# One weight tile in four split by ScalarE and an accumulating DMA, and two small reorderings, in an encoder layer on one core

## The chip, the cores and the metric

The kernel runs on one core of one Trainium2 chip. The metric is the device time of one execution in microseconds (us), the median of three runs. TensorE is called PE below, its weight loads PEld, VectorE DVE, ScalarE ACT, GpSimd POOL and SyncE SP. SP issues the plain DMAs.

## The reference, cut to what matters

The program is one layer of a bidirectional encoder, run on a prompt of 512 tokens and a sample of 256, each behind 16 meta tokens, with a model width of 1024, all in float32:

```python
h = h + 0.5 * swiglu(rmsnorm(h, ffn1_norm_w), ffn1_w_gate, ffn1_w_up, ffn1_w_down)   # width 2816
u = rmsnorm(h, mix_norm_w)
q, k, v, z, xbc, dt = split(u @ w_in)
h = h + concat([diff_attention(q, k, v), ssd_mixer(z, xbc, dt)]) @ w_out
h = h + 0.5 * swiglu(rmsnorm(h, ffn2_norm_w), ffn2_w_gate, ffn2_w_up, ffn2_w_down)
return rmsnorm(h, final_norm_w)[meta tokens dropped]
```

`diff_attention` has 8 heads with two score maps each; `ssd_mixer` is a chunked state-space scan in both directions over chunks of 128 tokens.

## The kernel before, in words

**Float32 by three products.** PE multiplies float32r, a rounded float32. So every operand is kept as a big part `hi` (the rounded value) and a small part `lo` (what the rounding left), and a product is the sum of three matmuls, hi·hi, lo·hi and hi·lo, in that order (`mm3`, lines 320 to 322). `split` (lines 184 to 186) makes the two parts of a weight tile: ACT casts the raw tile into `hi` (L185), DVE subtracts `hi` from the raw tile into `lo` (L186).

**Weights.** They stream from HBM through the class `Weights`. A raw tile `wr` is 512 rows by 256 columns, stored as 128x1024 (512 KB), in two buffers, loaded by SP (L212). Its two parts lie in `wh` and `wl`, four buffers each. `jobs` is the list of splits in the order of use; `pump` makes one further split whenever a buffer has been freed.

**The feed-forward layers** are cut into groups of column pairs (`GROUPS`). The first group is computed plainly. In each later one `quad` computes a 2x2 block product by seven products of quarter size in place of eight; a quad is run for the gate weights and one for the up weights of each pair of column tiles. Its four weight jobs are `a` (one quarter), `b` and `d` (sums of quarters, made by DVE in the tile `sums`, L258 to L264, before their split) and `c` (the second raw tile as it is). The products run as p1 (needs `a`), then p4 of the quad before, p6 and p5 (need `b`), p2 (needs `c`), p7 and p3 (need `d`), and p4 (needs `c` again), which is put off behind the next quad's p1. One product is 12 matmuls of 392 columns (384 in the second layer). After each group `down` adds its part of the down projection.

**Between the layers** the input projection runs, and beside it, in a generator advanced a step at a time between the projection's matmuls, the state-space scan (`seq`, from line 1178). Each of its rounds, two to a chunk, loads three 512 KB tiles of rows of `ar_d` spread over the partitions (`load_ab`, L1212 and L1216), masks two on POOL (L1236), takes exponentials on ACT (L1240, L1241), three elementwise passes on DVE (L1243 to L1245), and multiplies on PE (L1253, L1256). The tiles come from the pool `w4` of 15 buffers, which the scan shares with its states, its transposed inputs and the rest of the stage.

**Parameters.** The generator `parameters` waits 30 rounds, loads 18 small pieces by SP (L854 to L863), waits 4 rounds, transposes the packed vectors on PE (L876), and multiplies and sums the four lambda vectors on DVE (L880, L881).

**What sets the order.** The framework's planner orders each engine's queue at build time: instructions have their priority from the program's order, and one that is ready early by the planner's own estimate of times may be put ahead of others. On the chip each engine then works through its queue in that fixed order. `behind(ins)` ties instructions to come after `ins` on the same engine.

Of the kernel before, what the change touches and what calls it, by code (L numbers as in the profile page):

```python
# [10 lines left out]
AF = mybir.ActivationFunctionType  # L11
ALU = mybir.AluOpType
PSUM = bass.MemoryType.PSUM

P = 128
# [24 lines left out]
LAM_INIT = 0.8 - 0.6 * math.exp(-0.0)  # L40
# [7 lines left out]
def body(tc, x_prompt, x_sample, meta_tokens, ffn1_norm_w, ffn1_w_gate, ffn1_w_up, ffn1_w_down,  # L48
# [3 lines left out]
    nc = tc.nc  # L52
    V = nc.vector
    S = nc.scalar
    G = nc.gpsimd
# [51 lines left out]
    def ps_x():  # L107
        return pp.tile([P, 512], F32, tag="x", name="ps_x", bufs=2)
# [10 lines left out]
    ident = const.tile([P, P], F32, name="ident")  # L119
# [15 lines left out]
    raws_in = []  # L135
    jobs = []
# [44 lines left out]
            plan_1(("o", part, cp), w_out0, k0, 4, 256 * cp, 256)  # L181
    plan_ffn(2, ffn2_w_gate[0], ffn2_w_up[0], ffn2_w_down[0])

    def split(hi, lo, src):
        a = S.copy(hi, src)  # L185
        return a, V.tensor_tensor(lo, src, hi.bitcast(F32), ALU.subtract)  # L186

    @contextmanager
    def behind(ins):

        with ExitStack() as st:
            for i in ins:
                st.enter_context(tc.issue_after(i.ins))
            yield
# [5 lines left out]
    class Weights:  # L200
        raw, ready = {}, {}
# [42 lines left out]
        def split_fast(self, key, kind, raw, hi, lo):  # L244

            x, y = slice(0, P), slice(P, 2 * P)
            if kind == "c":
                ins = split(hi, lo, raw[0])
                self.ready[key] = [[(hi[:, i, c], lo[:, i, c]) for i in range(4)] for c in (x, y)]
                return ins  # L250
            hv, lv = (t.rearrange("p a b -> p (a b)").rearrange("p (s k f) -> p s k f", s=2, k=4) for t in (hi, lo))
            if kind == "a":
                ins = split(hv[:, 0], lv[:, 0], raw[0][:, :, x])
            else:
                if kind == "b":
                    sums = stretch_pool[0].tile([P, 2 * 4 * P], F32, tag="sums", name="sums", bufs=1)
                    t = self.sums = sums.rearrange("p (s k f) -> p s k f", s=2, k=4)
                    V.tensor_tensor(t[:, 1], raw[0][:, :, y], raw[1][:, :, y], ALU.add)  # L258
                    V.tensor_tensor(t[:, 0], t[:, 1], raw[0][:, :, x], ALU.add)
                else:  # L260

                    t, self.sums = self.sums, None
                    V.tensor_tensor(t[:, 1], raw[0][:, :, x], raw[0][:, :, y], ALU.add)
                    V.tensor_tensor(t[:, 0], t[:, 0], raw[1][:, :, x], ALU.add)  # L264
                ins = split(hv, lv, t)
            self.ready[key] = [[(hv[:, q, i], lv[:, q, i]) for i in range(4)] for q in range(1 if kind == "a" else 2)]
            return ins
# [45 lines left out]
            done()  # L313

    last_mm = [None]

    def mm3(ps, a, b, start, stop, onto=False):

# [180 lines left out]
    def ffn(f, h, halves, norm, after, last, new_g, new_up, first, parts=None, rms=None, ended=None):  # L499
# [145 lines left out]
        def d_unit(ws, k0, m, part):  # L645
            o, n = part
            ps = ps_any()
            dense(ps[:, :n], ws, m % 2, [g_t[k0 + i] for i in range(len(ws))], o, n)
            dst = h[m][:, o:o + n]
            V.scalar_tensor_tensor(dst, ps[:, :n], 0.5, dst, ALU.mult, ALU.add)  # L650

        def down(g):
            k0 = 2 * bounds[g]
# [134 lines left out]
    ps = ps_s()[:, 0, :]  # L788
# [7 lines left out]
    for js in ((0, 1, 2), (3, 4, 5), (6, 7)):  # L796
        ps = (ps_x if js[0] == 3 else ps_mm)()
# [4 lines left out]
        with behind([a]):  # L802
            for j in js:
                ins = put_h(js[0] == 3, j, at[j - js[0]], 0, C0)
# [47 lines left out]
    def parameters():  # L852
        def rep(dst, src, n):
            nc.sync.dma_start(out=dst, in_=src.partition_broadcast(n))  # L854

        for _ in range(30):
            yield 1
        V.memset(prm, 0.0)
        for (src, n), a in zip(rows, offs):
            nc.sync.dma_start(out=prm[a:a + n, :], in_=src.rearrange("(k p) -> k p", p=P))  # L860
        nc.sync.dma_start(out=prm[cw0:cw0 + 70, :], in_=conv_w[0].rearrange("t (k p) -> (t k) p", p=P))
        nc.sync.dma_start(out=prm[sub0:sub0 + 1, :], in_=attn_subln_w[0:1])
        nc.sync.dma_start(out=rbT, in_=rel_bias.rearrange("b h -> h b"))  # L863
        for j in range(2):
            rep(dvec[64 * j:64 * j + 64, :], ssm_d[0].rearrange("(m j) -> j m", j=2)[j], 64)
        rep(dtb[:, 0:16], dt_bias_fwd[0], P)
        rep(dtb[:, 16:32], dt_bias_bwd[0], P)
        rep(nega[:, 0:16], a_log_fwd[0], P)
        rep(nega[:, 16:32], a_log_bwd[0], P)
        lqk = [small([P, P], "B", 4).rearrange("p (i d) -> p i d", i=2) for _ in range(2)]  # L870
        for i, src in enumerate((lambda_q1, lambda_k1, lambda_q2, lambda_k2)):
            rep(lqk[i // 2][:, i % 2, :], src[0], P)
        for _ in range(4):
            yield 1
        ps = ps_x()
        nc.tensor.transpose(ps[:, :P], prm, ident)  # L876
        V.tensor_copy(prmT, ps[:, :P])
        V.tensor_scalar(subw, prmT[:, sub0:sub0 + 1], 1.0 - LAM_INIT, None, ALU.mult)
        for i in range(2):
            V.tensor_tensor(lqk[i][:, 0, :], lqk[i][:, 0, :], lqk[i][:, 1, :], ALU.mult)  # L880
            V.reduce_sum(lam2[:, i:i + 1], lqk[i][:, 0, :], mybir.AxisListType.X)  # L881
        yield 1

    def distances():
# [291 lines left out]
    def seq(chunks, meta_col):  # L1176
# [31 lines left out]
        def load_ab(c, g):  # L1208
            ab = []
            for d in range(2):  # L1210
                t = w4(D).rearrange("p (h t) -> p h t", h=8)
                nc.sync.dma_start(out=t, in_=ar_d[d, 8 * g:8 * g + 8, P * c:P * c + P].partition_broadcast(P))  # L1212
                ab.append(t)
            ea = w4(D).rearrange("p (h t) -> p h t", h=8)
            for d in range(2):
                nc.sync.dma_start(out=ea[64 * d:64 * d + 64],  # L1216
                                  in_=ar_d[d, 8 * g:8 * g + 8, P * c:P * c + P].partition_broadcast(64))
            ab_q.append((ab, ea))

        for i, c in enumerate(chunks):  # L1220
            col = CH[c]
            kk = 128 if i < L - 1 else 64
            X = Xs[c]
            ps = ps_s()
            for g in range(2):
                nc.tensor.matmul(ps[:, g, :P], xbc[8][64 * g:64 * g + 64, col:col + P],
                                 xbc[9][64 * g:64 * g + 64, col:col + P], start=True, stop=True)
            cb = ssm["row"][:, 416:672].rearrange("p (g t) -> p g t", g=2)
            S.copy(cb, ps[:, :, :P])
            for g in range(2):  # L1230
                load_ab(c, g)
                yield 1
                ab, ea = ab_q.pop(0)
                for d in range(2):
                    step = 1 - 2 * d
                    G.affine_select(out=ab[d], in_=ab[d], compare_op=ALU.is_ge, fill=NEGBIG, base=0,  # L1236
                                    pattern=[[0, 8], [step, P]], channel_multiplier=-step)
                    for h in range(8):
                        col_s = 16 * d + 8 * g + h
                        S.activation(ab[d][:, h, :], ab[d][:, h, :], AF.Exp, bias=ssm["asp"][:, c, col_s:col_s + 1])  # L1240
                S.activation(ea, ea, AF.Exp)  # L1241
                yield 1
                V.tensor_tensor(ea, ea, ssm["cdup"][g][:, col:col + P].unsqueeze(1).to_broadcast([P, 8, P]), ALU.mult)  # L1243
                V.tensor_tensor(ab[0], ab[0], ab[1], ALU.add)
                V.tensor_tensor(ab[0], ab[0], cb[:, g, :].unsqueeze(1).to_broadcast([P, 8, P]), ALU.mult)  # L1245
                yield 1
                ps = ps_x()
                for j in range(4):
                    o = [ps[64 * e:64 * e + 64, j * P:(j + 1) * P] for e in range(2)]
                    for e in range(2):  # L1250
                        h = 2 * j + e
                        hh = 8 * g + h
                        nc.tensor.matmul(o[e], X[:, 64 * hh:64 * hh + 64], ab[0][:, h, :], start=True, stop=False)  # L1253
                    for e in range(2):
                        h = 2 * j + e
                        nc.tensor.matmul(o[e], H[i][:kk, g, 64 * h:64 * h + 64], ea[:kk, h, :], start=False, stop=True)  # L1256
                for j in range(4):
                    m = 4 * g + j
                    V.scalar_tensor_tensor(xbc[m][:, col:col + P], xbc[m][:, col:col + P], dvec[:, m:m + 1],
                                           ps[:, j * P:(j + 1) * P], ALU.mult, ALU.add)  # L1260
# [450 lines left out]
```

## Time and profile before

| | |
|---|---|
| median of 3 runs (lowest to highest) | 1845.69 us (1845.63 to 1845.99) |
| the profiled execution | 1846.13 us |
| its span, first to last instruction | 1844.4 us |
| mean granted PE clock | 0.988 |
| PE busy, PEld busy | 97%, 93% of the span |
| DVE, ACT, POOL busy | 70%, 43%, 5% |
| DMA | 169.75 MB, mean 92 GB/s |

The span is cut by stages in the windows below. Matmuls overlap in the record, so a matmul shows some 340 ns of its own while the next one starts 0.17 to 0.18 us later; what PE loses shows as idle time before an instruction and in the granted clock.

### The profile page before, as it was taken

Reading aid. Unit: us, or ns where it says so; the run is one execution under the profiler, and the core shown is the slowest. Engines: PE = TensorE matmul, PEld = TensorE weight load, DVE = VectorE, ACT = ScalarE, POOL = GpSimd, SP = SyncE. Lnnn points to the kernel's source line nnn. Section 1 sums busy time; section 2 is a strip of 40 time slices with the busy share of each in tenths; the row PEclk is TensorE's granted clock in tenths of the full one; section 3 lists DMA queues with packets and bytes.
Section 4 is the critical chain, followed back from the end, with each engine's and each line's share of the span. In section 5 each row is a group of like instructions: output and inputs, shape, how many; then the busy total and the mean of one; then the engine's idle time right before and its main releaser. Section 6 shows DMA issues by size and latency. Waiting matters only on the chain.

```text
span 1844.4 us, 27371 instructions
## 1 busy us (share of the span) xinstructions
PE 1790.5 (97%) x10718; PEld 1719.0 (93%) x10718; DVE 1296.1 (70%) x2511; ACT 797.8 (43%) x1564; POOL 93.8 (5%) x118
## 2 busy tenths in 40 slices
PE   7999999999999999999899999999999999999998
PEld 6999999999998898878899898999999999999997
DVE  6857858686766697667788888674877575757573
ACT  5523414232333453668367676343433232424244
POOL 0000000000011000224100000001100000000002
PEclk8999999999999999999899999999999999999999
DMA  4212222212222523877431325321123121212121
GB/s 144 69 46 69 65 73 58 80 58 76 59 88 91 164 73 114 221 200 216 152 99 60 101 77 190 99 101 32 35 80 91 46 90 47 89 45 87 47 79 69
DMA packets 161268, 169.75 MB, mean 92 GB/s; under 512 B 9921, under 2 KB 146234, under 8 KB 161138
## 3 DMA queue, kind: packets, MB, share of 16 engines
q1 hardware_dynamic: 161122, 168.00, 30.3%
q8 instruction: 84, 1.38, 0.3%
q14 instruction: 46, 0.38, 0.1%
q10 hardware_dynamic: 16, 0.00, 0.0%
HBM read 148.54 MB, written 22.87 MB: 93 GB/s over the span
## 4 chain that ended last, share of the span: by engine, by line
PE 78%; DVE 11%; ACT 4%; DMA 4%; issue 2%; SPq 1%; POOL 0%; DVEq 0%; POOLq 0%; ACTq 0%
PE ps_mm L320 12%; PE ps_mm L322 11%; PE ps_mm L321 11%; PE ps_x L320 8%; PE ps_x L322 8%; PE ps_x L321 8%; PE ps_s L320 4%; PE ps_s L321 4%; PE ps_s L322 4%; DVE w L1056 2%; PE ps_s L1493 2%; DVE wl L186 2%; ACT w L1240 1%; PE ps_s L1611 1%; DMA w<-ar_d 1%
## 5 line engine op out<-in xcount | busy, mean ns | idle before, releaser
L320 PE MATMUL ps_mm<-w,wh 128*128 128x384 f32 (+3 forms) x1296 | 441.1, 340 | 5.2 <-ACT w L185 2.1
L321 PE MATMUL ps_mm<-w,wl 128*128 128x384 f32 (+3 forms) x1296 | 438.7, 338 | 1.7 <-DVE wl L186 1.7
L322 PE MATMUL ps_mm<-w,wh 128*128 128x384 f32 (+3 forms) x1256 | 426.2, 340 | 2.8 <-DVE w L186 2.2
L185 ACT CAST wh<-wr 128x1024 fp32r<-128x1024 f32 (+1 forms) x194 | 182.4, 941 | 218.6 <-PE ps_x L322 141.3
L320 PEld LDWEIGHTS ps_mm<-w,wh 128*128 128x128 f32 x1296 | 244.7, 189 | 11.9 <-ACT w L185 3.0
L321 PEld LDWEIGHTS ps_mm<-w,wl 128*128 128x128 f32 x1296 | 244.8, 189 | 4.9 <-DVE wl L186 2.3
L322 PEld LDWEIGHTS ps_mm<-w,wh 128*128 128x128 f32 x1256 | 237.2, 189 | 7.3 <-DVE w L186 3.0
L186 DVE TENSOR_TENSOR wl<-wr,wh 128x1024 fp32r<-128x1024 f32 (+1 forms) x194 | 212.4, 1095 | 41.4 <-ACT wh L185 39.7
L185 ACT CAST wh<-sums 128x1024 fp32r<-128x1024 f32 x76 | 79.8, 1051 | 212.4 <-PE ps_x L322 129.2
L320 PE MATMUL ps_x<-w,wh 128*128 128x392 f32 (+4 forms) x496 | 169.2, 341 | 0.9 <-ACT w L1138 0.9
L321 PE MATMUL ps_x<-w,wl 128*128 128x392 f32 (+4 forms) x496 | 167.2, 337 | 0.0
L322 PE MATMUL ps_x<-w,wh 128*128 128x384 f32 (+4 forms) x456 | 153.7, 337 | 0.0
L186 DVE TENSOR_TENSOR wl<-sums,wh 128x1024 fp32r<-128x1024 f32 x76 | 93.1, 1225 | 50.4 <-ACT wh L185 50.4
L185 ACT CAST w<-w 128x384 fp32r<-128x384 f32 (+4 forms) x110 | 63.6, 579 | 122.1 <-DVE w L576 62.5
L369 POOL TENSOR_TENSOR w<-w,w 128x392 f32<-128x392 f32 (+3 forms) x36 | 41.7, 1159 | 1466.2 <-ACT w L368 1088.7
L650 DVE SCALAR_TENSOR_TENSOR w<-ps_x,w 128x392 f32<-128x392 f32 (+3 forms) x96 | 53.8, 560 | 82.8 <-PE ps_x L322 82.5
L320 PE MATMUL ps_s<-w,wh 128*128 128x384 f32 (+1 forms) x304 | 103.3, 340 | 1.7 <-DVE f L603 0.8
L321 PE MATMUL ps_s<-w,wl 128*128 128x384 f32 (+1 forms) x304 | 103.0, 339 | 0.0
L322 PE MATMUL ps_s<-w,wh 128*128 128x384 f32 (+1 forms) x304 | 102.9, 338 | 0.0
L320 PEld LDWEIGHTS ps_x<-w,wh 128*128 128x128 f32 x496 | 95.4, 192 | 2.0 <-ACT w L1138 1.2
L321 PEld LDWEIGHTS ps_x<-w,wl 128*128 128x128 f32 x496 | 95.3, 192 | 0.7
L650 DVE SCALAR_TENSOR_TENSOR w<-ps_mm,w 128x392 f32<-128x392 f32 (+3 forms) x96 | 53.6, 558 | 59.1 <-PE ps_mm L322 58.8
(372 smaller groups left out, 3776.0 us busy)
## 6 DMA issues: line engine op xcount, KB each, us to landing
wr<-in_ffn_w_gate_dram SPq DMA_DIRECT2D x44, 512.0 KB
wr<-in_ffn_w_up_dram SPq DMA_DIRECT2D x42, 512.0 KB
wr<-in_w_in_dram SPq DMA_DIRECT2D x42, 512.0 KB
wr<-in_ffn_w_down_dram SPq DMA_DIRECT2D x40, 512.0 KB
w<-ar_d SPq DMA_DIRECT2D x24, 512.0 KB
wr<-in_w_out_dram SPq DMA_DIRECT2D x16, 512.0 KB
w<-ar_d SPq DMA_DIRECT2D x24, 256.0 KB
w<-q_d SPq DMA_DIRECT2D x32, 192.0 KB
```

What stands on the lines that cost most here:

```text
L185: a = S.copy(hi, src)
L186: return a, V.tensor_tensor(lo, src, hi.bitcast(F32), ALU.subtract)
L320: nc.tensor.matmul(ps, ah, bh, start=start, stop=False, skip_group_check=onto)
L321: nc.tensor.matmul(ps, al, bh, start=False, stop=False, skip_group_check=onto)
L322: last_mm[0] = nc.tensor.matmul(ps, ah, bl, start=False, stop=stop, skip_group_check=onto)
L369: G.tensor_tensor(sums[0], sums[0], sq, ALU.add)
L650: V.scalar_tensor_tensor(dst, ps[:, :n], 0.5, dst, ALU.mult, ALU.add)
L1056: V.scalar_tensor_tensor(acc, pad[:, j:j + XW], prmT[:, cw:cw + 1], acc, ALU.mult, ALU.add)
L1240: S.activation(ab[d][:, h, :], ab[d][:, h, :], AF.Exp, bias=ssm["asp"][:, c, col_s:col_s + 1])
L1493: nc.tensor.matmul(ps[:, b, :w], qh[c][part][:, P * i:P * i + P], kh[c][:, k0 + b * w:k0 + b * w + w], start=part == 0, stop=part == 1)
L1611: nc.tensor.transpose(ps[:n, 0, q * P:(q + 1) * P], A[q0 + q][:, c:c + n], ident)
```

## The change

`split_dma` makes the parts of job `c` without DVE: ACT casts the raw tile into `hi`, ACT then writes the rounded negative of the raw tile into `lo`, and a DMA issued by POOL adds the same weights, read again from HBM, into `lo`. The other jobs are split as before. `last_down` remembers the last DVE instruction of the down projection. `parameters` waits 60 rounds in place of 30 and 16 in place of 4, and its DVE work is tied behind `last_down`. In `seq` the loads of the next round stand one round earlier in the program.

```diff
+    def split_dma(hi, lo, src, again):
+
+        S.copy(hi, src)
+        S.activation(lo, src, AF.Copy, scale=-1.0)
+        G.dma_start(out=lo, in_=again, accum_op=ALU.add)
+
...
             if kind == "c":
-                ins = split(hi, lo, raw[0])
+                src, k0, nk, c0, ncol = raws_in[jobs[self.n_split][2][0]]
+                ins = split_dma(hi, lo, raw[0], src[k0 * P:(k0 + nk) * P, c0:c0 + ncol].rearrange("(k p) f -> p k f", p=P))
...
-            V.scalar_tensor_tensor(dst, ps[:, :n], 0.5, dst, ALU.mult, ALU.add)
+            last_down[0] = V.scalar_tensor_tensor(dst, ps[:, :n], 0.5, dst, ALU.mult, ALU.add)
...
-        for _ in range(30):
+        for _ in range(60):
             yield 1
...
-        for _ in range(4):
+        for _ in range(16):
             yield 1
-        ps = ps_x()
-        nc.tensor.transpose(ps[:, :P], prm, ident)
...
+        with behind([last_down[0]]):
+            ps = ps_x()
+            nc.tensor.transpose(ps[:, :P], prm, ident)
...
+        order = [(c, g) for c in chunks for g in range(2)]
+        load_ab(*order[0])
         for i, c in enumerate(chunks):
...
             for g in range(2):
-                load_ab(c, g)
+                if (c, g) != order[-1]:
+                    load_ab(*order[2 * i + g + 1])
                 yield 1
```

## Rows read from the trace of the kernel before

**Rows 1.** The page: busy time of the engines in us, share of the span, instructions.
```profile
PE 1790.5 (97%) x10718; PEld 1719.0 (93%) x10718; DVE 1296.1 (70%) x2511; ACT 797.8 (43%) x1564; POOL 93.8 (5%) x118
```

**Rows 2.** Busy time by windows: the two stretches of quads and the scan. Columns: window, its length, busy us (instructions) of each engine, granted clock, DMA share, GB/s.
```profile
100.00:540.00 440.00, 439.42 (x2460) 437.36 (x2459) 312.05 (x492) 135.68 (x191) 5.14 (x5) 1.00 0.23 68
730.00:885.00 155.00, 143.56 (x1030) 125.55 (x1027) 104.60 (x137) 111.16 (x263) 43.87 (x32) 0.96 0.77 208
1390.00:1800.00 410.00, 409.69 (x2330) 407.45 (x2329) 264.50 (x396) 131.82 (x184) 0.00 (x0) 1.00 0.23 70
```

**Rows 3.** What PE waited for over the whole span: us in total, times, longest us.
```profile
PE ps_x L1253 <- DVE w L1245: 8.7, 3, 3.7
PE ps_x L357 <- DVE w L349: 7.3, 4, 5.3
...
PE ps_x L1253 <- ACT w L1240: 2.7, 1, 2.7
```

**Rows 4.** The timeline of the start, from 30 to 42 us, PE, DVE and ACT. Columns: start, duration, engine, line, instruction, in brackets the idle time before it and what ended it.
```profile
30.59 0.29 PE L322 MATMUL ps_x<-w,wh 128*128 128x272 f32 x1
...
34.52 0.22 DVE L880 TENSOR_TENSOR B<-B 128x64 f32<-128x64 f32 x1 [4.22 <-DMA B<-in_lambda_k_dram]
36.03 0.23 DVE L880 TENSOR_TENSOR B<-B 128x64 f32<-128x64 f32 x1 [1.29 <-DMA B<-in_lambda_k_dram]
36.31 0.43 DVE L541 TENSOR_TENSOR w<-ps_x,w 128x272 f32<-128x272 f32 x1
...
37.10 1.05 ACT L750 ACTIVATE w<-w 128x1024 f32<-128x1024 f32 x1
...
41.27 0.47 DVE L349 TENSOR_SCALAR w<-ident,xrr 128x128 f32<-128x128 f32 x2
...
41.60 1.22 PE L357 MATMUL ps_x<-w,ones 128*128 128x128 f32 x4 [5.31 <-DVE w L349]
```

**Rows 5.** The chain that ended last, in its piece at the start: start, duration, what.
```profile
19.25 13.42 DMA dvec<-in_ssm_d_dram
...
33.06 2.88 DMA B<-in_lambda_k_dram
```

**Rows 6.** Windows of the start, columns as in rows 2.
```profile
36.30:41.60 5.30, 0.00 (x0) 0.00 (x1) 4.02 (x21) 2.48 (x6) 0.00 (x0) 0.89 0.01 2
41.60:47.30 5.70, 5.70 (x27) 5.70 (x28) 3.69 (x10) 5.10 (x14) 0.00 (x0) 0.51 0.01 3
```

**Rows 7.** The instructions that use the raw weight tiles `wr`: count, least, median and greatest ns, first and last start.
```profile
L258 DVE TENSOR_TENSOR sums<-wr x38: 682/692/694, 106.3 to 1769.4; 128x512 f32<-128x512 f32 x38
```

**Rows 8.** The timeline of a quad that follows another one, all engines, columns as in rows 4.
```profile
383.23 0.34 PE L320 MATMUL ps_s<-w,wh 128*128 128x392 f32 x1
...
383.47 1.05 ACT L185 CAST wh<-wr 128x1024 fp32r<-128x1024 f32 x1 [0.31 <-PE ps_mm L322]
...
384.76 1.22 DVE L186 TENSOR_TENSOR wl<-wr,wh 128x1024 fp32r<-128x1024 f32 x1
...
386.01 0.37 SPq L212 DMA_DIRECT2D wr<-in_ffn_w_gate_dram  x1
...
391.79 0.34 PE L320 MATMUL ps_s<-w,wh 128*128 128x392 f32 x1
...
391.97 0.34 PE L321 MATMUL ps_s<-w,wl 128*128 128x392 f32 x1
...
398.20 0.34 PE L320 MATMUL ps_s<-w,wh 128*128 128x392 f32 x1
```

**Rows 9.** DMAs of 512 KB on the chain that ended last, in the second feed-forward layer and in the scan: start, us to landing, what.
```profile
1364.32 4.04 DMA wr<-in_ffn_w_up_dram
...
1378.89 5.48 DMA wr<-in_ffn_w_gate_dram
...
773.11 9.39 DMA w<-ar_d
```

**Rows 10.** The timeline of the scan, PE and SP: the last matmuls of a round, the loads issued then, and two of PE's waits.
```profile
751.38 0.39 PE L1256 MATMUL ps_x<-w,w 128*64 128x128 f32 x4
...
751.96 1.27 SPq L1212 DMA_DIRECT2D w<-ar_d  x2
...
769.47 0.44 PE L1253 MATMUL ps_x<-w,w 128*64 128x128 f32 x4 [3.43 <-DVE w L1245]
...
790.83 0.44 PE L1253 MATMUL ps_x<-w,w 128*64 128x128 f32 x4 [2.70 <-ACT w L1240]
```

**Rows 11.** Windows of the scan, columns as in rows 2.
```profile
790.00:800.00 10.00, 9.17 (x64) 8.87 (x65) 8.84 (x12) 7.49 (x23) 3.63 (x3) 0.83 0.75 192
```

**Rows 12.** The timeline of the first quad of a group, ACT and PE, columns as in rows 4.
```profile
361.97 1.05 ACT L185 CAST wh<-wr 128x1024 fp32r<-128x1024 f32 x1 [7.50 <-PE ps_x L322]
...
372.42 0.34 PE L320 MATMUL ps_mm<-w,wh 128*128 128x392 f32 x1
373.16 0.44 PE L320 MATMUL ps_s<-f1s,wh 128*128 128x392 f32 x1
...
376.82 0.34 PE L320 MATMUL ps_s<-w,wh 128*128 128x392 f32 x1
```

**Rows 13.** The timeline of the scan, DVE: the same operation on the same shape, first with POOL idle, then beside POOL's mask.
```profile
754.43 1.22 DVE L1243 TENSOR_TENSOR w<-w,w 128x1024 f32<-128x1024 f32 x1
...
765.19 2.11 DVE L1243 TENSOR_TENSOR w<-w,w 128x1024 f32<-128x1024 f32 x1
```

## The prediction on record

> **What bounds the kernel now.** I read the page's busy times first: PE is busy for 1790.5 of 1844.4 us [rows 1], so at most 54 us of idle time and whatever the clock withholds can be won at all. Next I cut the span into windows, since an average over stages says nothing of one. In both stretches of quads PE is full: it lacks 0.6 of 440 us and 0.3 of 410 us, at full clock, while DVE has a quarter to a third of the time to spare [rows 2]. So work taken from DVE there wins nothing by itself. PE's waits then name the places where time is lost: the scan, where it waits for DVE's last pass and for ACT's exponentials, and the start, with one wait of 5.3 us for L349 [rows 3]. Last I followed the start in the timeline and in the chain. DVE stands 4.22 us and another 1.29 us at L880, the product of the lambda vectors, until these have landed [rows 4]; they come late behind a load of `ssm_d` that holds the chain for 13.42 us [rows 5]. What is queued behind L880 on DVE is L541, whose matmuls had started their last at 30.59; behind that ACT's L750, the chain of the second norm, L349, and PE's L357 at 41.60 after 5.31 us of idling. The granted clock then falls to 0.51 for the 5.7 us that follow [rows 6], which is the lower level, 1.2 GHz.
>
> **Part 1, the parameters.** The DVE work at L880 is tied behind a down projection, so it no longer heads DVE's queue at 34 us. L541 can go at about 31.0, when its matmuls have ended, in place of 36.31: 5.3 us earlier. ACT's L750 must first finish its first call and a cast (1.05 and 0.42 us each), so I let the chain come 5.1 us earlier, and L357 would be ready at 41.60 - 5.1 = 36.5, where PE has been free since 36.3 [rows 4, 6]. The wait falls from 5.3 to about 0.3 us: 5.0 us. Without that gap the half clock should go too: 5.7 x (1 - 0.51) = 2.8 us [rows 6]. What is late next is the same chain for the third block, whose squares and norm do not get faster with PE; the other three waits of this kind come to 2.0 us, 0.7 us each [rows 3], and I take one such back. Sum: 5.0 + 2.8 - 0.7 = 7.1 us won, between 4.3 (half clock stays) and 7.8. The PE transpose and the few DVE operations behind it go to the quads, where DVE has 128 of 440 us free [rows 2]. The loads themselves stay on SP in the planner's hands; nothing on PE waits for them before the norm after the first layer. Should the planner still put them early, they cost as they do now, nothing in PE's time once L880 is out of the way.
>
> **Part 2, the split of `c`.** There is one `c` job to a quad, 38 in all [rows 7]. Each takes one subtraction of 1.22 us from DVE (46 us in all) and adds to ACT a pass like the cast beside it, 1.05 us (40 us in all) [rows 8]. ACT is busy for 136 of 440 us there, so this hides, and DVE's gain hides nothing that was open [rows 2]: both 0. What counts is when `lo` is ready. In a quad behind another one the cast of `c` starts at 383.47, when p3 of the quad before has ended, and now `lo` is complete at 384.76 + 1.22 = 385.98. PE wants `hi` at 391.79 and `lo` at 391.97, its second matmul of p2 [rows 8]. So there are 6.0 us to spare today. After the change ACT has written the negative at 383.47 + 2 x 1.05 = 385.57, and POOL's DMA has 6.40 us from there to land. Behind that wait on POOL nothing is queued: POOL works 5 of 440 us there, and 0 of 410 in the second stretch [rows 2]. But PE's queue stands behind the wait for `lo`, and it is the engine without slack.
>
> The trace of before has no DMA of POOL and none that adds. The nearest rows are SP's plain loads of the same 512 KB, which land 4.04 to 5.48 us after they are issued; in the crowded scan one of 512 KB took 9.39 us [rows 9]. Between these lies the limit of 6.40 us. At the lower end the cost is 0 with 0.9 us to spare. At the upper end PE waits 3.0 us per quad, and by the scan's wait of 2.70 us, after which a slice of 10 us was granted 0.83 [rows 10, 11], up to 1.7 us more for the clock. The second raw load of the next quad is issued at 386.01, the moment the old subtraction lets its buffer go [rows 8], and so will fall together with the new DMA, which speaks for more than 5.5 us. Three things speak for less than a full wait. First, 10 of the 38 quads are the first of their group (five groups in each layer); there `c` is cast at 361.97 and wanted at 376.82 [rows 12], so 28 are exposed. Second, the planner moves PE's work: in that quad four matmuls of p5 run at 372.42 ahead of p6 [rows 12]; p7 or p3 put ahead of p2 would give 2.1 us each, a seventh of the 14.97 us from one p1 to the next [rows 8]. Third, the DMA share is 0.23 in this stretch [rows 2], so the engines have room. I take 0 by the plain loads of the same stage and keep 28 x 4.7 = 132 us as the far end; below nothing I find at most 1 us, what PE lacks in the two stretches together.
>
> The Trainium skill (DMA: Bandwidth & Descriptors, Anatomy of one DMA, SWDGE path) puts a DMA issued by POOL at 2.0 us plus its bytes over 436e3 per us, an estimate of 3.2 us for 512 KB; the sum by it is the same 0 for this part. The trace does not agree: even SP's plain loads take 4.04 us and more [rows 9], so the margin is a quarter of what that page leaves.
>
> **Part 3, rows one round ahead.** PE's waits at 769.47 and 790.83 (3.43 and 2.70 us) and the slice at 0.83 (1.7 us) stand behind rounds whose loads came late [rows 9, 10, 11]: if both went, 7.8 us would be won. But the loads of the third round are issued at 751.96, right as PE's last matmuls of the first round (751.38) let its tiles go [rows 10]. So they already run as far ahead as the 15 buffers of `w4` allow, and the program's order is not what holds them. Taking three tiles earlier can also starve another user of the pool: one more wait as long as the longest, 3.7 us [rows 3], in each of the two scans would cost 7.4 us. Between -7.8 and +7.4 the row at 751.96 is the nearest to the case: 0.
>
> **Sum.** 1846.1 (the profiled execution) - 7.1 + 0 + 0 = 1839.0 us. That execution lies 0.4 us above the median of the runs, so the prediction is 1838.6 us.
>
> **The rivals.** *`lo` comes late, slower.* Place: the second matmul of p2 in 28 quads. It decides from the point where POOL's DMA takes over 6.40 us. For it: the meeting with the raw load, and that a sum has to fetch what is already in `lo` besides the weights; against it: the plain loads and the planner's freedom. Halfway between 6.40 and 9.39 us PE waits 1.5 us: 28 x 1.5 = 42 us, so 1838.6 + 42 = 1881 us. A wait of 0.25 us per quad already eats the gain of part 1.
>
> Of the same place, with another cause: POOL and DVE hinder each other in this kernel. L1243 takes 1.22 us with POOL idle and 2.11 us beside POOL's mask [rows 13]. If POOL's preparation of the DMA is held up by DVE's passes, the DMA starts later by one of 1.22 us; from plain loads of 5.48 us that makes 6.7 us, 0.3 us late, 28 x 0.3 = 8 us, and the time 1847 us. The Trainium skill (SBUF — State Buffer, SBUF: two separate sides) has such a rule: DMAs issued from GpSimd starve of descriptors while DVE runs a copy that uses both ports. By it the quads are nearly safe, since their DVE work is of two-input operations; no row here shows a POOL DMA beside one.
>
> *The start's gain does not arrive, no change.* If the planner puts something else that waits into DVE's queue at 31 us, or if part 3 starves the pool by what part 1 wins, the time is 1845.7 - 7.1 + 7.1, about 1846 us. For it: L880 was itself such a piece of early work; against it: it alone waited for a DMA there.
>
> **How the numbers follow.** The forecast 0.52, with 1830 to 1843 as its own range (7.8 and 7.8 us won at best; 4.3 won at the start with a little lost in the scan at worst). `lo` late 0.28 at 1881; late by DVE's hindrance 0.06 at 1847; no change 0.14 at 1846. This kernel's runs lie within 0.4 us of each other, and a difference over 0.2%, 3.7 us, can be told from none. From the forecast 0.50 is faster and 0.02 the same; the late cases give 0.31 slower, 0.03 the same; the third case gives 0.03 faster, 0.08 the same and 0.03 slower. So faster 0.53, same 0.13, slower 0.34. The range reaches from 1830, both gains in full, to 1890, which is 1.8 us of waiting per exposed quad; beyond it I leave 0.12 above and 0.06 below.
>
> **What would show it.** Part 1: no wait on a DMA at L880 before 100 us, L357 near 36.5 us and no half clock after it. Part 2: PE idle before L321 in p2, with POOL's DMA as the releaser, or none; the time from the end of ACT's second pass to that DMA's landing against 6.40 us; p7 standing ahead of p2 if the planner moved it. Part 3: when L1212 is issued against the end of the round before last, and the waits at L1253. The prediction is wrong if the quads lengthen beyond 14.97 us, or if the half clock at 42 us stays without the gap.

## The result, and the profile after

The changed kernel takes 1871.2 us (1868.3 to 1873.4), the kernel before 1845.7 us: a ratio of 1.0138, with an interval of 1.0123 to 1.0153. So it is slower by 25.5 us; 1838.6 us had been forecast. The profiled execution has a span of 1869.1 us.

**The start came as forecast.** The timeline after, columns as in [rows 4], and the same two windows as in [rows 6]:

```profile
30.68 0.44 DVE L549 TENSOR_TENSOR w<-ps_x,w 128x272 f32<-128x272 f32 x1 [0.60 <-PE ps_x L330]
...
31.48 1.06 ACT L758 ACTIVATE w<-w 128x1024 f32<-128x1024 f32 x1
...
36.00 0.71 PE L365 MATMUL ps_x<-w,ones 128*128 128x128 f32 x4
```

```profile
36.30:41.60 5.30, 5.30 (x47) 5.30 (x46) 4.79 (x13) 5.30 (x15) 0.00 (x0) 1.00 0.01 3
41.60:47.30 5.70, 5.28 (x45) 5.11 (x44) 3.86 (x19) 2.21 (x6) 0.00 (x0) 1.00 0.00 0
```

L549 (L541 before) goes at 30.68 in place of 36.31, L365 (L357 before) at 36.00 in place of 41.60; PE is busy where it idled for 5.3 us, and the clock of 0.51 behind it is 1.00.

**The quads lost far more.** The three windows of [rows 2], after:

```profile
100.00:540.00 440.00, 434.17 (x2411) 428.06 (x2410) 287.49 (x467) 149.07 (x206) 27.70 (x23) 1.00 0.37 87
730.00:885.00 155.00, 145.78 (x1028) 127.46 (x1026) 103.16 (x138) 112.20 (x263) 41.54 (x32) 0.97 0.75 206
1390.00:1800.00 410.00, 396.59 (x2228) 391.73 (x2228) 232.99 (x362) 137.53 (x189) 21.83 (x17) 0.99 0.38 88
```

PE lacked 0.6 and 0.3 us in the stretches of quads; now it lacks 5.8 and 13.4 us. What it waits for there is named by its waits and by DVE's over the whole span (us in total, times, longest):

```profile
PE ps_s L328 <- DVE f L611: 9.0, 4, 2.9
PE ps_s L329 <- DMA wl<-in_ffn_w_up_dram: 6.9, 10, 1.3
PE ps_s L329 <- DMA wl<-in_ffn_w_gate_dram: 5.1, 7, 1.4
PE ps_s L328 <- DVE w L611: 3.6, 2, 2.4
...
PE ps_x L365 <- DVE w L357: 0.9, 2, 0.4
```

```profile
DVE sums L265 <- DMA wr<-in_ffn_w_gate_dram: 28.6, 14, 4.2
```

Two kinds of wait stand there: 12.0 us in 17 times at L329, the second matmul of p2, for POOL's transfer into `lo`; and 12.6 us in 6 times at L328, for L611, which is DVE's evacuation of p6. Before, PE never stood for `lo` at that place, and for the evacuation (then L603) 1.7 us in 4 times:

```profile
PE ps_s L320 <- DVE f L603: 0.8, 1, 0.8
PE ps_s L320 <- DVE w L603: 0.7, 2, 0.4
...
PE ps_s L320 <- DVE f1t L603: 0.2, 1, 0.2
```

The page gives the transfer's time from issue to landing in its last column:

```profile
wl<-in_ffn_w_gate_dram POOLq DMA_DIRECT2D x19, 512.0 KB, 7.6
wl<-in_ffn_w_up_dram POOLq DMA_DIRECT2D x19, 512.0 KB, 7.7
```

**The first kind, in the timeline of one quad:**

```profile
396.64 1.06 ACT L187 ACTIVATE wl<-wr 128x1024 fp32r<-128x1024 f32 x1 [0.24 <-PE ps_mm L329]
...
397.60 1.04 ACT L186 CAST wh<-wr 128x1024 fp32r<-128x1024 f32 x1
...
397.99 1.28 POOL L188 DMA_DIRECT2D wl<-in_ffn_w_gate_dram  x1 [13.95 <-ACT wl L187]
...
398.66 0.37 SPq L218 DMA_DIRECT2D wr<-in_ffn_w_up_dram  x1
...
405.17 0.34 PE L328 MATMUL ps_s<-w,wh 128*128 128x392 f32 x1
...
406.27 0.44 PE L329 MATMUL ps_s<-w,wl 128*128 128x392 f32 x1 [0.76 <-DMA wl<-in_ffn_w_gate_dram]
```

The planner put the negative ahead of the cast, as in 33 of the 38 quads, so POOL issues at 397.99, 0.29 us behind the negative's end. Without a wait the second matmul of p2 would have started 0.18 us behind the first, as in [rows 8]: at 405.35, which is 7.36 us after the issue (an estimate). The page's 7.6 us is a median, and a transfer that takes that long is late by some 0.3 us; the one of this quad landed after 8.2 us, and L329 starts at 406.27, 0.9 us late. SP's raw load is issued 0.67 us behind POOL's transfer.

**The second kind, in the second quad of a group** (four of the six are there, the other two in first quads):

```profile
1477.80 1.28 POOL L188 DMA_DIRECT2D wl<-in_ffn_w_up_dram  x1 [20.01 <-ACT w L524]
...
1478.73 0.37 SPq L218 DMA_DIRECT2D wr<-in_ffn_w_gate_dram  x1
...
1486.02 0.69 DVE L265 TENSOR_TENSOR sums<-wr 128x512 f32<-128x512 f32 x1 [3.67 <-DMA wr<-in_ffn_w_gate_dram]
1486.63 0.55 DVE L611 TENSOR_TENSOR f<-f,ps_s 128x384 f32<-128x384 f32 x1
...
1487.23 0.69 PE L328 MATMUL ps_s<-w,wh 128*128 128x384 f32 x1 [2.39 <-DVE f L611]
```

Here the raw load needs 7.3 us beside the transfer (1478.73 to 1486.02). DVE's sum for the next quad, L265, stands for it at the head of DVE's queue; behind it stands L611; and p2 writes into one half of the PSUM tile whose other half L611 reads, so PE stands for 2.39 us. The matmul after the gap takes 0.69 us in place of 0.34: the lower clock level, 1.2 GHz. The trace has three such stretches of 3.4 us in the quads, from 1371.0, 1487.1 and 1586.0 us, where before had none; all three are at waits of this second kind, none at a wait for `lo`. DVE already stood for such a load before, but for less, with 2.2 us as the longest:

```profile
DVE sums L258 <- DMA wr<-in_ffn_w_gate_dram: 18.6, 14, 2.2
```

The loss can be added up from this: 12.0 + 12.6 us of waits, half of 3 x 3.4 us at half the clock, 5.1 us, and for each of the 23 waits the 0.16 us by which two matmuls overlap in the record, 3.7 us: some 33 us (an estimate). The changed kernel is 33.6 us slower than the same without the split (e2 below).

### The profile page after: what moved, and what is told of

The parts are those of the page before. It is cut to its first block, busy times and chain, and to the rows that moved or that the text cites. A ratio compares the mean times of both kernels' runs of the same rounds, so it can differ in the third digit from the quotient of the medians.

```text
span 1869.1 us, 27465 instructions
## 1 busy us (share of the span) xinstructions
PE 1801.9 (96%) x10718; PEld 1723.7 (92%) x10718; DVE 1253.2 (67%) x2473; ACT 828.6 (44%) x1602; POOL 140.4 (8%) x156
## 5 line engine op out<-in xcount | busy, mean ns | idle before, releaser
L328 PE MATMUL ps_mm<-w,wh 128*128 128x384 f32 (+3 forms) x1296 | 442.4, 341 | 5.1 <-ACT w L191 2.0
L329 PE MATMUL ps_mm<-w,wl 128*128 128x384 f32 (+3 forms) x1296 | 439.6, 339 | 1.6 <-DVE wl L192 1.6
L328 PEld LDWEIGHTS ps_mm<-w,wh 128*128 128x128 f32 x1296 | 245.6, 190 | 12.1 <-ACT w L191 3.0
L329 PEld LDWEIGHTS ps_mm<-w,wl 128*128 128x128 f32 x1296 | 245.6, 190 | 4.9 <-DVE wl L192 2.2
L191 ACT CAST wh<-wr 128x1024 fp32r<-128x1024 f32 (+1 forms) x156 | 142.5, 914 | 151.5 <-PE ps_x L330 79.3
L192 DVE TENSOR_TENSOR wl<-wr,wh 128x1024 fp32r<-128x1024 f32 (+1 forms) x156 | 164.7, 1056 | 37.0 <-ACT wh L191 35.2
L328 PE MATMUL ps_x<-w,wh 128*128 128x392 f32 (+4 forms) x496 | 167.9, 338 | 0.9 <-ACT w L1148 0.9
L329 PE MATMUL ps_x<-w,wl 128*128 128x392 f32 (+4 forms) x496 | 166.2, 335 | 0.0
L329 PE MATMUL ps_s<-w,wl 128*128 128x384 f32 (+1 forms) x304 | 106.9, 352 | 12.3 <-DMA wl<-in_ffn_w_up_dram 6.9
L328 PE MATMUL ps_s<-w,wh 128*128 128x384 f32 (+1 forms) x304 | 104.9, 345 | 12.6 <-DVE f L611 9.0
L328 PEld LDWEIGHTS ps_x<-w,wh 128*128 128x128 f32 x496 | 94.1, 190 | 2.0 <-ACT w L1148 1.2
L329 PEld LDWEIGHTS ps_x<-w,wl 128*128 128x128 f32 x496 | 94.2, 190 | 0.7
L330 PEld LDWEIGHTS ps_x<-w,wh 128*128 128x128 f32 x456 | 86.6, 190 | 0.7
```

The costliest lines, as they stand in the source:

```text
L328: nc.tensor.matmul(ps, ah, bh, start=start, stop=False, skip_group_check=onto)
L329: nc.tensor.matmul(ps, al, bh, start=False, stop=False, skip_group_check=onto)
L330: last_mm[0] = nc.tensor.matmul(ps, ah, bl, start=False, stop=stop, skip_group_check=onto)
```

## The experiments

For the stages, the table shows by how much four instructions of each trace come earlier (-) or later (+) than in the trace of before, in us. A: the last of ACT's passes `b12`, which prepare the activations for the quads (98 us before). B: the first square of the norm behind the first layer's quads (530 us). C: the first difference that prepares the second layer (1326 us). D: the first pass of the last norm (1800 us).

```
                            A       B       C       D
after                     -8.0    +0.7    -1.1   +24.2
e1, part 2 alone          -1.0    +6.1    +7.2   +31.9
e2, parts 1 and 3         -7.7    -7.9    -7.8    -9.0
e3, part 1 alone          -8.0    -7.4    -7.8    -8.7
e4, part 3 alone          -1.1    -1.4    -2.0    -3.2
e5, spare transfer        -8.2    -7.5    -8.7    -9.9
e6, plain copy            -8.2    -8.2   -11.2   -11.3
e7, no transfer           -8.1    -8.7   -15.4   -17.5
e8, p2 behind p7 and p3   -7.7    -8.8    -8.2   -10.7
e10, sum behind p6        -7.9    +3.2    +5.5   +21.5
e11, transfer halved      -8.5    -8.6    -9.5    -1.8
e12, e10 and e11          -7.9    -8.0   -11.2   -13.7
```

The -1.0 of e1 and e4 at A, where they are the kernel before, shows how far a single trace is to be trusted. So does the way from B to C, the mixer: the ten kernels with the rows one round ahead have the same source there, and their shift changes by +2.3 (e10) to -6.7 (e7), on average by -1.4; in e1 and e3, without it, by +1.1 and -0.3. What is not in the quads is read with that in mind.

### e1 to e4: the parts apart

**e1**, part 2 alone: `parameters` and `seq` as before.

> Part 2 alone, on the kernel before. Theory (the split of `c` carries the whole loss: PE waits for `lo` at its second matmul of p2, and DVE's sum of the next quad waits for the raw load that was issued beside POOL's DMA): the stretches of quads lose what they lost in the changed kernel, 8.7 us in 100 to 540, 5.2 us in 1300 to 1400 and 17.8 us in 1400 to 1800, so 1845.7 + 32 = 1877 us, between 1872 and 1882. Rival (the split costs nothing by itself; the loss comes from parts 1 and 3, which shift the planner's order): 1844 to 1848 us.

1877.14 us, ratio 1.0177 (1.0160 to 1.0193). The split by itself is slower by 31.6 us: 7.1 of them from A to B and 24.8 from C to D, the two stretches of quads, and 1.1 between. The theory's time came, and the rival fell.

**e2**, parts 1 and 3:

```diff
-                src, k0, nk, c0, ncol = raws_in[jobs[self.n_split][2][0]]
-                ins = split_dma(hi, lo, raw[0], src[k0 * P:(k0 + nk) * P, c0:c0 + ncol].rearrange("(k p) f -> p k f", p=P))
+                ins = split(hi, lo, raw[0])
```

> Parts 1 and 3 without the split. Theory (the split carries the whole loss; the start won 6.2 us and the scans 4.8 us by the gaps on PE): 1845.7 - 11 = 1835 us, between 1833 and 1838, and faster than both kernels. Rival (the loss comes from the order that parts 1 and 3 leave): 1865 us or more. Second rival (part 3's gain in the scan is a by-product of the DVE work that the split took away): 1839 us, part 1 alone.

1837.56 us, ratio 0.9955 (0.9940 to 0.9970): faster than both kernels. It lies at the edge of the theory's range, and nearer to the second rival; the rival that put the loss on parts 1 and 3 fell.

**e3**, part 1 alone (also without the loads one round ahead):

> Part 1 alone. Theory (the wait at the start and the half clock behind it go, and nothing else moves): 1845.7 - 6.5 = 1839 us, between 1837.5 and 1841.5. Rival (what is won at the start is given back by another late chain): 1844 to 1847 us.

1836.27 us, ratio 0.9957 (0.9943 to 0.9971): 9.3 us faster by the medians, 5.4 to 10.5 by the interval, and 1.2 us under the theory's range. The start's share is read at A: 8.0 earlier, against 1.0 where nothing was changed, so 7.0 us. The rest came later, where the program is that of before, and within the scatter of the traces.

**e4**, part 3 alone (`parameters` as before and no split).

> Part 3 alone. Theory (the rows' loads come earlier in both scans, PE's gaps there fall by some 5 us as in the changed kernel): 1841 us, between 1839 and 1843. Rival, the one on record with the prediction (the buffers of `w4` hold the loads, so the program's order changes nothing): 1845.7 us, within 1.5.

1841.23 us, ratio 0.9980 (0.9970 to 0.9990): 4.3 us faster by the medians, 1.8 to 5.5 by the interval: the theory's time, and not the rival's. Its reason is shown only in part. The timeline of SP in the scan and of PE's first long wait there:

```profile
734.01 2.94 SPq L1221 DMA_DIRECT2D w<-ar_d  x2
...
751.53 0.39 PE L1268 MATMUL ps_x<-w,w 128*64 128x128 f32 x4
...
751.77 1.70 SPq L1221 DMA_DIRECT2D w<-ar_d  x2
...
768.16 0.44 PE L1265 MATMUL ps_x<-w,w 128*64 128x128 f32 x4 [2.00 <-DVE w L1257]
```

The second round's load, at 741.14 before, is issued 7.1 us earlier. The third round's is still issued right behind the last matmuls of the first round, at 751.77 against 751.96 in [rows 10]: it is the buffers that hold it. PE's wait fell from 3.43 to 2.00 us, and its waits at this line over the whole scan from 11.4 us [rows 3] to 8.9. That is half of the theory's 5 us, and between B and C, where the scan lies, this trace gains 0.6 us. Beside part 1 the gain can't be found: e2 and e3 ran together and differ by 1.3 us the other way.

### e5 to e8: what in the split costs time

**e7**, no transfer:

```diff
-        G.dma_start(out=lo, in_=again, accum_op=ALU.add)
```

> The changed kernel without POOL's transfer: ACT still makes both passes, and `lo` of `c` then holds the negative of the weights, so the small part of that tile is left out. Theory (the transfer alone carries the loss, by its late landing and by the raw load that it delays): all 33 us between the changed kernel and parts 1 and 3 alone are gone, 1838 us, between 1834 and 1841, and no wait at the second matmul of p2. Rival (ACT's second pass, and the order that the planner makes of it, cost time of their own): 1848 us or more.

1833.41 us, ratio 0.9942 (0.9924 to 0.9960), 0.6 us under the theory's range. The whole loss is gone: ACT's second pass and the planner's new order cost nothing that shows. Whether the DVE work that is gone wins something here stays open: the time is 4.2 us under e2's, but the intervals of the two ratios overlap. PE is full in the second layer:

```profile
1390.00:1800.00 410.00, 410.00 (x2313) 1.00 0.21 66
```

(Here the columns are the window, its length, PE's busy time, the granted clock, the DMA share and GB/s.)

**e6**, the transfer as a plain copy:

```diff
-        G.dma_start(out=lo, in_=again, accum_op=ALU.add)
+        G.dma_start(out=lo, in_=again)
```

> The changed kernel with POOL's transfer as a plain copy of the same 512 KB, so `lo` of `c` holds the weights themselves and the product is another. Theory (what makes the transfer late is that POOL issues it and that it meets the raw load; the adding is the smaller share): landing still 6.5 us or more after the issue, and 1858 to 1871 us. Rival (the adding makes it late, since it also has to fetch what is in `lo`): landing 5.5 us or less after the issue, and 1838 to 1846 us.

1838.12 us, ratio 0.9973 (0.9960 to 0.9986), and the theory fell: the rival was right. The page's row of the transfer:

```profile
wl<-in_ffn_w_gate_dram POOLq DMA_DIRECT2D x19, 512.0 KB, 4.3
```

SP's raw load is issued as far behind POOL's as before (0.67 or 1.1 us), the transfer goes through the same queue and moves the same bytes, and it lands in 4.3 us in place of 7.6. So 3.3 us of the 7.6 are due to the adding, and they are the difference between hidden and late. But they are not all spent on adding. POOL's own work falls too, from 1.28 to 0.74 us, and the two transfers change places: POOL's first packet comes 1.5 us after its issue (a median), ahead of SP's, where in the changed kernel it came after 3.9, mostly behind SP's. From first to last packet it is 2.4 us in place of 3.5. One transfer of each trace, the first of the second layer, has the raw load 1.6 us behind it; there the adding one lands after 5.9 us and the copy after 4.1. By this pair the adding without the meeting is worth 1.9 us (5.93 - 4.06), and the rest of the 3.3 comes from the meeting.

**e8**, p2 behind p7 and p3:

```diff
-            return [p1, p6, p5, p2, p7, p3, p4]
+            return [p1, p6, p5, p7, p3, p2, p4]
```

(with the request for `c` moved to the head of p7, so that the weights are taken in the order of the splits).

> The changed kernel with p2, the first user of `c`, moved behind p7 and p3, so `lo` has some 4 us more to land. Theory (two mechanisms: the late `lo`, 16 us of waits at the second matmul of p2, and the late raw load, some 15 us with its half clock): the first goes and the second stays, 1871 - 16 = 1855 us, between 1848 and 1860, with the waits of 2 to 3 us behind DVE's sum still there in the second quads. Rival (the late `lo` alone is the loss, the waits behind the raw load are its echo): 1838 to 1844 us. Second rival (p7 has to wait for `d` instead): 1868 us or more.

1836.18 us, ratio 0.9956 (0.9939 to 0.9972). It lies under the theory's range and both rivals'. The transfer still lands 7.4 to 7.5 us after its issue, and in the second layer the raw loads beside it still take some 6.4 to 6.6 us to their last packet where POOL's go first, but no wait of p2 is left. I had taken this edit to separate the two kinds of wait. It doesn't: p2 waits for `lo` and for L611 alike, and both get the 4 us.

**e5**, the transfer with nobody waiting, in the second layer:

```diff
-        S.activation(lo, src, AF.Copy, scale=-1.0)
-        G.dma_start(out=lo, in_=again, accum_op=ALU.add)
+        if second[0]:
+            spare = stretch_pool[0].tile([P, 3, 256], F32R, tag="spare", name="spare", bufs=1)
+            S.activation(spare, src[:, :3], AF.Copy, scale=-1.0)
+            G.dma_start(out=spare, in_=again[:, :3], accum_op=ALU.add)
+        V.tensor_tensor(lo, src, hi.bitcast(F32), ALU.subtract)
```

> Parts 1 and 3, with DVE's subtraction as before; in the second layer alone ACT's negative and POOL's adding transfer are made as well, into a spare tile that nobody reads, and of 384 KB (three of the four blocks) for want of room. Theory (the transfer costs time even when nobody waits for it, because the raw load issued beside it comes late and DVE's sum stands at the head of DVE's queue): waits of 2 to 3 us remain at some five second quads of the second layer and a half clock behind them, 1837.6 + 13 = 1850 us, between 1843 and 1856. Rival (only the wait for `lo` costs time): 1836 to 1840 us.

1832.95 us, ratio 0.9943 (0.9925 to 0.9962): no loss, and a time under the rival's range as well. But this run doesn't speak against the second kind of wait, since it missed its case: with DVE's subtraction back, the raw tile comes free at another time, and in all the transfers no raw load is issued within 4 us behind POOL's. It tells something else. Alone, 384 KB land in 5.2 us, with the first packet 2.0 us and the last 4.9 us after the issue. By these 512 KB would have their last packet at 2.0 + 2.9 x 4/3 = 5.9 us (an estimate), which PE's 7.4 us would have covered. The changed kernel has one transfer nearly alone, the one at 1359.44 us named under e6: its packets run from 2.0 to 5.6 us and it lands after 5.9. Where SP's raw load runs first, the first packet comes after some 4.0 us. So the late `lo` needs both, the adding and the meeting.

### e10 to e12: the two kinds of wait taken away, alone and together

**e10**, DVE's sum tied behind the evacuation of p6 of the quad before (`last_p6`):

```diff
-                    V.tensor_tensor(t[:, 1], raw[0][:, :, y], raw[1][:, :, y], ALU.add)
+                    with behind([last_p6[0]] if last_p6[0] else []):
+                        V.tensor_tensor(t[:, 1], raw[0][:, :, y], raw[1][:, :, y], ALU.add)
```

> The changed kernel with DVE's sum of the next quad put behind the evacuation of p6 on DVE's queue, so that a late raw load no longer holds p2. Theory (two mechanisms of their own: PE's waits for `lo`, and its waits for that evacuation, which come to 12.6 us in the changed kernel's rows, with a half clock behind them): the second goes, the first stays, 1871 - 17 = 1854 us, between 1848 and 1860. Rival (the waits behind the evacuation are an echo of the late `lo`): 1866 us or more.

1866.48 us, ratio 1.0121 (1.0093 to 1.0149): 4.7 us better than the changed kernel by the medians, and so nearer to the rival. The two ratios' intervals overlap, so by itself this gain is not clear of noise. PE's waits (the lines are two greater):

```profile
PE ps_s L331 <- DMA wl<-in_ffn_w_up_dram: 11.5, 16, 1.6
...
PE ps_s L331 <- DMA wl<-in_ffn_w_gate_dram: 9.6, 8, 2.3
...
PE ps_s L330 <- DVE w L613: 0.5, 1, 0.5
```

The waits for the evacuation are gone, 12.6 to 0.5 us, and those for `lo` have grown from 12.0 to 21.1 us: where PE had stood for DVE, it now mostly stands for the transfer. No half clock is left in the quads.

**e11**, the transfer in two halves, the columns that p2 reads first:

```diff
-        G.dma_start(out=lo, in_=again, accum_op=ALU.add)
+        for c in (slice(0, P), slice(P, 2 * P)):
+            G.dma_start(out=lo[:, :, c], in_=again[:, :, c], accum_op=ALU.add)
```

> The changed kernel with POOL's transfer cut in two, the 128 columns that p2 reads first and those that only p4 reads behind them. Theory (the late `lo` is a mechanism of its own, and its time goes with the bytes): the first half lands near 4.0 + 3.4 / 2 = 5.7 us after its issue, PE's waits at the second matmul of p2 go, those behind the late raw load stay: 1855 us, between 1848 and 1860. Rival (the time goes with the number of packets, of which the first half has as many): landing at 7 us or more, 1868 us or more.

1845.35 us, ratio 1.0007 (0.9997 to 1.0017): 25.8 us better than the changed kernel, more than either theory gave. By its packets the first half is complete 5.6 us after its issue, and it lands after 6.05 (medians of 38). PE waits for `lo` once, and what is left is the other kind (the lines are one greater):

```profile
PE ps_s L329 <- DVE f L612: 4.2, 5, 2.1
...
PE ps_s L329 <- DVE w L612: 2.8, 2, 2.6
...
PE ps_s L330 <- DMA wl<-in_ffn_w_gate_dram: 0.4, 1, 0.4
```

In the table the first layer has lost nothing and the second 7.8 us (C to D).

**e12**, both edits:

> Both of the two edits together: the sum behind the evacuation of p6 and the transfer in two halves. Theory (two mechanisms, and the two together are the whole loss): 1838 us, between 1834 and 1843, like parts 1 and 3 alone. Rival (something else in the transfer costs time, such as its load on the DMA engines or POOL): 1848 us or more.

1834.60 us, ratio 0.9948 (0.9931 to 0.9966). Nothing of the loss is left, with POOL's transfers, their 19.9 MB and the DMA share all there:

```profile
1390.00:1800.00 410.00, 410.00 (x2313) 1.00 0.40 89
```

So both kinds are real, and they cover each other. e10, e11 and e12 were measured together: from e10 to e12 the late `lo` is worth 31.9 us, from e11 to e12 the sum in front of the evacuation 10.8 us, both clear of noise. Taken away alone from the changed kernel, which was measured at another time, the first is worth 25.8 us by the medians (24 by the ratios), the second 4.7 us (3 by the ratios, not clear of noise); both together 36.6 us (35 by the ratios). And the split, freed of both, buys nothing that can be told from noise: e12, e8, e2 and e3 lie between 1834.6 and 1837.6 us, each from its own few runs.

## Why the prediction was wrong

**The step that failed** is in part 2: "I take 0 by the plain loads of the same stage". The price of the adding transfer was bounded by 4.04 and 9.39 us, and the value came from SP's loads of the same bytes [rows 9]. It measured 7.6 us, and e6 shows why the row was the wrong neighbour: a plain copy by POOL does land in 4.3 us, as those rows say, but the adding costs 3.3 us more beside the raw load, some 1.9 us of them without it. The text had the mechanism among the rival's reasons (a sum "has to fetch what is already in `lo`") and gave it no price of its own.

**The Trainium skill's estimate** (DMA: Bandwidth & Descriptors, Anatomy of one DMA, SWDGE path), 3.2 us for 512 KB, is 1.1 us under the plain copy of e6 and less than half of the adding transfer; the forecast's warning that even plain loads took longer was right, and no reason to take 0.

**The rival "`lo` comes late"** is what came, with a chance of 0.28 and 1881 us, 10 us from the time. Its place, p2's second matmul, is right, but that its sum comes so near is in part luck: it has no second kind of wait, and its terms were mis-sized in both directions. The limit of 6.40 us assumed the cast ahead of the negative; the planner turned them round, and from the negative's end at 397.70 to 405.35 it was 7.65 us. The transfer landed 8.5 us after that end in the quad shown. PE's wait was not 1.5 us in 28 quads but 0.71 us in 17 named ones (12.0 / 17), 0.88 us in 24 once the other wait is out of the way (e10), and none of them had the half clock that the far end of 4.7 us a quad counts in. Of the three reasons for less than a full wait the first held: none of the 17 waits is in a first quad of a group. The second did not come: the planner didn't move p7 ahead of p2 (e8 did that by hand, and it removes the loss). The third, a DMA share of 0.23, did not keep the two transfers from holding each other up.

**What was not foreseen** is the second kind of wait. The forecast saw that the raw load would "fall together with the new DMA" and asked only what this does to the DMA. It does as much to the raw load: 6.2 to 7.4 us to its last packet where POOL's go first, against 3.2 to 3.5 us as a rule where it is alone. Who waits for that load could be read before: L258 waited for it 14 times [rows 7 for the line], and behind L258 on DVE's queue stands p6's evacuation, with p2 behind that.

**That DVE's time wins nothing by itself** stands as far as the runs go (e12, against e2 and e3): in the quads PE was full and stays full at best. *No change* (0.14) did not come either: the start's gain arrived, as e3 shows. *Late by DVE's hindrance* (0.06): POOL prepared in 1.28 us beside DVE's passes in each quad, and no run shows such a delay.

**Part 1** was right: 7.0 us at A in e3 against 7.1 forecast, L365 at 36.00 against 36.5, no half clock behind it, the waits of this kind down from 7.3 to 0.9 us in the changed kernel (2.2 in e3). The one given back for the third block (0.7) did not come.

**Part 3** was right in one half of its reason and nearly so in its size. The buffers hold the third round's load, as argued; the second round's did move, which the argument left out, and PE's wait fell by 1.4 us. Alone it measured 1.8 to 5.5 us, on top of part 1 nothing, from B to C some 1.6 us on average (-1.4 against +0.2, the mean of e1, e3 and before). What it is worth stays open within these few us. That also goes for the sentence that runs "lie within 0.4 us of each other": 17 runs of the kernel before spread from 1841.3 to 1847.9 us.

**The sum by the measured terms:** -7.0 for the start, +31.6 for the split (e1), between 0 and -4 for the rows: 1845.7 + 20.6 to 24.6 = 1866 to 1870 us, against 1871.2.

## What to carry to other kernels

Price a new kind of transfer by its own operation: when no row shows an accumulating DMA, a plain one of the same bytes is a lower bound, not a likely value, and in a queue without slack a few tenths of a microsecond too late are paid in every round. When a transfer moves to a buffer's release, look at both that meet there, and at who stands at the head of a queue for the other one. Work taken from an engine that isn't the bound wins nothing by itself; here the repairs (p2 later; halves and a sum behind) bring back what the split cost and no more.

## What the runs showed of the hardware

- An accumulating transfer of 512 KB from HBM, issued by POOL, lands 7.6 us after its issue beside a raw load (after), the same bytes copied 4.3 us (e6); with the raw load 1.6 us behind it is 5.9 and 4.1 us, one transfer each. POOL works 1.28 us for the first and 0.74 us for the second. Its packets of 1 KB take 102 ns each, those of the copy 61 ns (medians).
- The two transfers that meet don't simply share: where SP's load, issued 0.67 us later, gets its packets out first, its last one ends some 3.9 us after its issue and POOL's begin after 4.0 us; where SP's is issued some 1.1 us later, POOL's begin after 2.0 us and SP's load takes 6.2 to 7.4 us to its last packet (after).
- Halved by columns, the same bytes in twice as many packets of 512 B let the first half land at 6.05 us (e11) in place of 7.6 us for the whole, with as many packets in that half as in the whole: the time went more with the bytes than with the packets, which took 65 ns each in place of 102.
